# A two-layer SSD and attention network on one core: one block for all stages, ordered by the detailed simulator, and context products by twos

## The chip, the core and the metric

The program runs on one core of a Trainium2 chip. The core has a matrix engine (TensorE, PE in the profile, with its weight loads as PEld), a vector engine (VectorE, DVE), a scalar engine (ScalarE, ACT), a general engine (GpSimd, POOL) and SyncE (SP), which here only issues DMA. Each engine takes its instructions in the order in which the build put them and waits at semaphores for the others. The metric is the device time of one execution, in microseconds (us).

## The reference

The kernel computes two layers of a backbone for 1024 latent tokens and 256 context tokens of width 1024, in float32. Each layer modulates its normalised input (scale, shift and gate from a product with `ada_w`), mixes the tokens, adds the gated result, and does the same with a mixture of experts.

- Layer 0 mixes by a bidirectional state-space scan (SSD): `in_w` projects to a gate z, to x, B and C (a depthwise convolution of width 5 and SiLU behind it) and to step sizes dt. Over chunks of 128 tokens, forwards and backwards, each of 32 heads has `y = (C Bᵀ · decay) x + C · state`, and `state = decay · state + Bᵀ x`; the output is `rmsnorm((y + D x) · silu(z)) @ out_w`. B and C are shared by 4 heads each (8 groups).
- Layer 1 mixes by attention: 16 query heads over 4 key/value heads of width 64, normalised and rotated, softmax over all 1280 tokens for each block of 128 queries.
- The mixture: 16 experts choose their tokens by a router's softmax (128 latent tokens each, 32 context tokens each), and for them `(silu(x w1) · (x w3)) w2`, weighted and added back. Layer 1 has it for latent tokens only.

The output is the normalised latent stream.

## The kernel before

Large products use a three-part form. `mm3` (L54 to L56) multiplies a high and a low part of the operands, high x high, high x low, low x high, into one PSUM tile; the parts are made by a copy on ScalarE (L48, L716) and a subtraction on VectorE or GpSimd (L49, L717, L719). Small products (transposes, scores, the scan's states, context tokens) are done in plain float32 (two passes of the array, so a plain product has two records in the profile).

The stages follow each other in `run`: `constants`, `ssd`, `ssd_out`, `moe(0, True)`, `attn`, `moe(1, False)`. Which instruction stands where on an engine is decided by the language's scheduler, which takes the code in its written order and with that the dependences, the tile pools' buffers and its own costs.

*SSD.* `conv_tile` loads 128 columns of `in_w` (`w_raw`, L323), splits them (L325, L328), projects all tokens in three blocks of 256, 512 and 512 (`in_ps`, L54 to L56), copies them (L351, L352) and applies the convolution (L356) and SiLU (L361, L362). For each of the 8 groups there is one such tile of B, one of C and two of x; each of the two x tiles holds a pair of heads, so the scan runs 16 times (`core`). One run, called a head pair here, transposes x (L371, `xtm`), makes the backward states (L404, with steps on VectorE L390), and then, two chunks at a time: loads the decays' exponents (`Eb`, L413), masks them (GpSimd L416), takes exponentials (ScalarE, 8 of L421), adds and multiplies them (L424, L425); weights x (L378), makes the forward states (L437) with steps (L390); multiplies the entering states by C (`yo_ps`, L450), scales them (`yos`, L454) and adds both directions on GpSimd (L457); and sums the parts of y on TensorE (L465, L467) and stores (L471). Before the groups come the norms, the weights of the modulation (`adw`, L119) and the part that makes dt (L256, L261).

*Mixture 0.* For each expert and each of its three matrices `product` runs over four k (256 rows of the weights each). A k loads 1 MB into a ring of five raw buffers (`m_raw`, L650), splits it, and runs 12 three-part products into `acc` (L54 to L56). The 32 context tokens are multiplied by the raw weights in plain float32: `ctx_part`, 8 products into `cacc` (L690). Where neither the first nor the last product of the stage is meant, this comes at the end of every k. It is the last reader of the raw buffer.

*Attention.* A unit (`Pair`) is two heads by 128 queries; 64 units are written out in an interleaved order. `score` makes the scores of one head, 1024 columns in `S[hh]` and 256 in `S3` (L1129), the maxima (L1133, L1137, L1138) and two exponentials (L1139 for the 256, L1141 for the 1024). `flip` transposes the probabilities (L1150) and copies them (L1155 on ScalarE, L1153 on VectorE), `values` multiplies them (L1163), `close` brings the sums in (L1173 to L1180).

Of the kernel before, what the change touches and what calls it, by code (L numbers as in the profile page):

```python
# [40 lines left out]
class Net:  # L41
# [626 lines left out]
    def moe(self, i, ctx):  # L668

        nc, tc, A = self.nc, self.tc, self.A  # L670
# [6 lines left out]
        with tc.tile_pool(name="mo", bufs=1) as mp, \  # L677
# [9 lines left out]
            def ctx_product(acc, xc, raw, kp):  # L687
                for k in (2 * kp, 2 * kp + 1):
                    for q in range(4):
                        nc.tensor.matmul(acc[32 * q:32 * q + 32], xc[:, k], raw[:, k % 2, 256 * q:256 * q + 256],  # L690
                                         start=(k == 0), stop=(k == KT - 1))

            def product(m, e, xl, xc, done=None):

                acc = [pp.tile([P, 512], F32, name="acc", bufs=5 if ctx else 6) for _ in range(2)]
                cacc = pp.tile([P, 256], F32, name="cacc", bufs=1) if ctx else None
                raws = {}

                def ctx_part(kp):
                    ctx_product(cacc, xc, raws[kp], kp)  # L700
                first = ctx and (m, e) == (0, 0)

                early = ctx and (m, e) == (2, E - 1)
                late = None
                for kp in range(4) if early else ():
                    raws[kp] = self.moe_raw(i, m, e, kp)
                    ctx_part(kp)
                if early:
                    done(cacc)
                for kp in range(4):  # L710
                    n = D - (D if i and m + e == 0 and kp < 3 else share)
                    if not early:
                        raws[kp] = self.ahead.pop(0) if self.ahead else self.moe_raw(i, m, e, kp)
                    raw = raws[kp]
                    w = [wp.tile([P, 2, D], F32R, name=f"m_w{k}", bufs=3) for k in range(2)]
                    nc.scalar.activation(w[0], raw, AF.Copy)  # L716
                    nc.gpsimd.tensor_tensor(w[1][:, :, n:], raw[:, :, n:], w[0][:, :, n:].bitcast(F32), op=OP.subtract)  # L717
                    if n:
                        nc.vector.tensor_tensor(w[1][:, :, :n], raw[:, :, :n], w[0][:, :, :n].bitcast(F32), op=OP.subtract)  # L719
                    for kk in range(2):  # L720
                        k = 2 * kp + kk
                        for b in range(2):
                            self.mm3(acc[b], [h[:, k] for h in xl], [h[:, kk, 512 * b:512 * b + 512] for h in w],
                                     k == 0, k == KT - 1)
                    if first and kp == 1:
                        self.rt.pp, self.rt.tag = pp, "m_tr"
                        self.rt.finish_ctx(self.ctx_rank)
                        self.rk.release()
                        self.hlp = tc.alloc_tile_pool(name="hl", bufs=2, side="right")
                        self.wkvp = tc.alloc_tile_pool(name="wkv", bufs=1, side="right")  # L730
                        self.wkv = [self.wkvp.tile([P, KT, 512], F32R, name=f"wkv{k}") for k in range(2)]
                        self.prep = tc.alloc_tile_pool(name="pre", bufs=1, side="right")
                        late = gather_ctx(0)
                    elif ctx and not first and not early:
                        ctx_part(kp)
                if first:
                    xc = turn_ctx(late)
                    for kp in range(4):
                        ctx_part(kp)
                if done and not early:  # L740
                    done(cacc)
                if m < 2:
                    next(extra, None)
                return acc, cacc
# [18 lines left out]
            def gather_ctx(e):  # L763
                return fetch(mp.tile([32, D], F32, name="xgc"), 0, self.idxC[0:32, e:e + 1]) if ctx else None
# [7 lines left out]
            def turn_ctx(xgc):  # L772
                if xgc is None:
                    return None
                ps = pp.tile([P, KT, 32], F32, name="m_tr", bufs=2)
                for j in range(KT):
                    nc.tensor.transpose(ps[:, j], xgc[:, j * P:(j + 1) * P], self.ident[0:32, 0:32])
                xT = mp.tile([P, KT, 32], F32, name="xTc")
                nc.vector.tensor_copy(xT, ps)
                self.xT = xT  # L780
                return xT
# [29 lines left out]
            def finish(e, gT):  # L811

                y, _ = product(2, e, gT, None)
                fw = slot()[:, 0]
                nc.sync.dma_start(fw, rows(A["final_norm_w"], [0, P], [1, D]))
# [36 lines left out]
            def down(e, gT, gc):  # L852
                y, _ = product(2, e, gT, gc, (lambda yc: scatter_ctx(e, yc)) if ctx else None)
                yr = mp.tile([P, D], F32, name="yrow")
                for b in range(2):
                    hs = slice(512 * b, 512 * b + 512)
                    nc.vector.scalar_tensor_tensor(yr[:, hs], y[b], self.gL[:, e:e + 1], g2[:, hs],
                                                   op0=OP.mult, op1=OP.mult)
                nc.gpsimd.indirect_dma_start(
                    out=self.xs[1], out_offset=bass.IndirectOffsetOnAxis(ap=self.idxL[:, e:e + 1], axis=0),  # L860
                    in_=yr, in_offset=None, compute_op=OP.add)
# [8 lines left out]
            for e in range(E):  # L870
                nx = gather(e + 1) if e + 1 < E else None
                nxc = gather_ctx(e + 1) if 0 < e < E - 1 else None
                a, ac = product(0, e, x, self.xT)
                s = mp.tile([P, D], F32, name="s")
                for b in range(2):
                    nc.scalar.activation(s[:, 512 * b:512 * b + 512], a[b], AF.Silu)
                sc = None
                if ctx:
                    sc = mp.tile([P, 256], F32, name="s_c")
                    nc.scalar.activation(sc, ac, AF.Silu)  # L880
                if e == 0:
                    nxc = gather_ctx(1)
                g, gc = product(1, e, x, self.xT)
                for b in range(2):
                    nc.vector.tensor_tensor(s[:, 512 * b:512 * b + 512], s[:, 512 * b:512 * b + 512], g[b], op=OP.mult)
                if ctx:
                    nc.vector.tensor_tensor(sc, sc, gc, op=OP.mult)
                if ctx and e == E - 2:
                    self.qkv_weights(self.wkv, 2, mp, 2)
                if nx:  # L890
                    x = turn(nx)
                    turn_ctx(nxc)
                if gT:
                    down(e - 1, *gT)
                gT = turn_g(s), turn_gc(sc)
# [368 lines left out]
    def run(self):  # L1264
        nc, tc = self.nc, self.tc
        with ExitStack() as es:
            self.constants(es)
            self.xs, self.h2d = ([tc.dram_tile([n, D], F32, name=f"{nm}{n}") for n in (CTX, LAT)] for nm in ("xs", "h2"))
            self.ssd()
            self.ssd_out()  # L1270
            self.moe(0, True)
            self.attn()
            self.moe(1, False)
            self.rtp.release()


class Router:
# [183 lines left out]
```

## Time and profile before

| | us |
|---|---|
| three runs | 3951.53, 3958.86, 3960.98 (median 3958.86) |
| profiled execution | 3960.7 |
| its span in the trace | 3958.9 |

| engine | busy us | share of the span |
|---|---|---|
| TensorE | 3617.8 | 91% |
| VectorE | 2645.7 | 67% |
| ScalarE | 2030.6 | 51% |
| GpSimd | 1809.5 | 46% |

The stages, as read from the lines at work, are: 0 to 62 us norms and the first modulation; 62 to 140 dt; 140 to 1045 the groups of the SSD; 1045 to 1260 its gates; 1260 to 1525 its output and the router; 1525 to 2390 mixture 0; 2390 to 2595 the projections of the attention; 2595 to 3114 its units; 3114 to 3255 its output and the router; 3255 to 3340 the ranking; 3340 to 3900 mixture 1; then the end. A stage's own row says which engine works through it, and its idle time is the length less the busy time. Records of TensorE overlap a little (0.40 us long, 0.23 apart), so distances are taken from start to start.

### The profile page before, as it was taken

How to read it: one execution, taken by the hardware profiler on the slowest of the kernel's cores; microseconds unless marked ns; L12 is line 12 of the kernel's file. 1: busy time of each engine (PE TensorE's matmuls, PEld its weight loads, DVE VectorE, ACT ScalarE, POOL GpSimd, SP SyncE). 2: the span in 40 equal slices, each digit the busy share in tenths (PEclk: the TensorE clock that was granted, in tenths of full speed). 3: DMA queues.
4: the chain of work that ended last, by engine and by line, in shares of the span. 5: the costliest groups of instructions: out<-in, count | busy, mean ns of one | idle time of the engine just before them, and what ended most of it. 6: DMA issues, size and time to landing. Idle time of an engine off the chain costs nothing.

```text
span 3958.9 us, 56801 instructions
## 1 busy us (share of the span) xinstructions
PE 3617.8 (91%) x21153; PEld 2676.8 (68%) x21153; DVE 2645.7 (67%) x3877; ACT 2030.6 (51%) x3325; POOL 1809.5 (46%) x1370
## 2 busy tenths in 40 slices
PE   5998989999999998999999998999999874999997
PEld 3666777777787775666666666767777653777765
DVE  4777777777633367666666655556666577999988
ACT  4544445444433224554554545477777433777665
POOL 1245545545543224665566663221111123777786
PEclk7999999999999999999999999999999986999999
DMA  4333322222544336889988873100000335999994
GB/s 170 102 102 116 125 81 77 77 77 73 154 143 147 118 128 228 304 298 307 308 298 299 272 248 100 39 17 1 1 1 12 128 129 208 387 375 375 350 335 173
DMA packets 296357, 681.09 MB, mean 172 GB/s; under 512 B 24192, under 2 KB 150000, under 8 KB 289936
## 3 DMA queue, kind: packets, MB, share of 16 engines
q1 hardware_dynamic: 269520, 615.50, 44.5%
q0 software_dynamic: 12720, 39.33, 4.1%
q10 hardware_dynamic: 13840, 22.63, 1.7%
q8 instruction: 167, 2.74, 0.3%
q14 instruction: 110, 0.90, 0.1%
HBM read 611.95 MB, written 62.82 MB: 170 GB/s over the span
## 4 chain that ended last, share of the span: by engine, by line
PE 50%; DVE 15%; issue 7%; POOL 5%; DMA 4%; ACT 3%; SPq 0%; POOLq 0%; ACTq 0%; DVEq 0%
DVE m_w L719 6%; PE acc L54 5%; PE cacc L690 5%; PE pv L1163 4%; PE acc L55 4%; PE acc L56 4%; PE S L1129 4%; PE a_tr L1150 4%; POOL m_w L717 3%; PE in_ps L54 2%; PE in_ps L55 2%; PE in_ps L56 2%; PE o_ps L56 2%; PE o_ps L55 2%; PE o_ps L54 2%
## 5 line engine op out<-in xcount | busy, mean ns | idle before, releaser
L719 DVE TENSOR_TENSOR m_w<-m_raw,m_w 128x1792 fp32r<-128x1792 f32 (+1 forms) x381 | 877.1, 2323 | 323.3 <-ACT m_w L716 320.8
L717 POOL TENSOR_TENSOR m_w<-m_raw,m_w 128x256 fp32r<-128x256 f32 (+1 forms) x384 | 859.5, 2248 | 403.5 <-ACT m_w L716 401.4
L716 ACT ACTIVATE m_w<-m_raw 128x2048 fp32r<-128x2048 f32 x384 | 732.4, 1915 | 493.3 <-PE acc L56 210.1
L54 PE MATMUL in_ps<-hh,w 128*128 128x512 f32 (+1 forms) x1152 | 429.3, 373 | 9.9 <-DVE th L493 9.9
L55 PE MATMUL acc<-m_w,xl 128*128 128x512 f32 x1024 | 409.1, 400 | 19.0 <-DVE m_w L719 12.4
L56 PE MATMUL in_ps<-hh,w 128*128 128x512 f32 (+1 forms) x1152 | 425.5, 369 | 0.0
L55 PE MATMUL in_ps<-hl,w 128*128 128x512 f32 (+1 forms) x1152 | 424.4, 368 | 0.0
L54 PE MATMUL acc<-m_w,xl 128*128 128x512 f32 x1024 | 412.9, 409 | 2.6 <-ACT xl L48 1.7
L56 PE MATMUL acc<-m_w,xl 128*128 128x512 f32 x1024 | 401.8, 393 | 0.0
L421 ACT ACTIVATE Eb<-Eb,ebias 128x128 f32<-128x128 f32 x640 | 201.8, 391 | 191.0 <-POOL Eb L416 191.0
L1133 DVE TENSOR_REDUCE mx<-S 128x1 f32<-128x1024 f32 x128 | 155.7, 1217 | 183.5 <-PE S L1129 183.5
L328 POOL TENSOR_TENSOR w<-w_raw,w 128x512 fp32r<-128x512 f32 x96 | 151.5, 1596 | 253.8 <-ACT w L325 245.5
L54 PEld LDWEIGHTS acc<-m_w,xl 128*128 128x128 f32 x1024 | 192.8, 189 | 91.8 <-issue 42.9
L54 PEld LDWEIGHTS in_ps<-hh,w 128*128 128x128 f32 x1152 | 221.6, 192 | 47.5 <-issue 11.8
L56 PEld LDWEIGHTS in_ps<-hh,w 128*128 128x128 f32 x1152 | 221.2, 192 | 38.1 <-issue 12.8
L55 PEld LDWEIGHTS in_ps<-hl,w 128*128 128x128 f32 x1152 | 221.5, 192 | 36.8 <-issue 12.0
L55 PEld LDWEIGHTS acc<-m_w,xl 128*128 128x128 f32 x1024 | 193.7, 189 | 77.0 <-DVE m_w L719 26.5
L1180 POOL TENSOR_TENSOR q<-s 64x128 f32<-64x128 f32 x128 | 57.6, 450 | 405.9 <-DVE mx L1138 338.0
L56 PEld LDWEIGHTS acc<-m_w,xl 128*128 128x128 f32 x1024 | 193.5, 189 | 40.2 <-DVE xl L49 0.2
L55 PE MATMUL acc<-m_w,gT 128*128 128x512 f32 x512 | 205.3, 401 | 6.6 <-DVE m_w L719 4.1
L54 PE MATMUL acc<-m_w,gT 128*128 128x512 f32 x512 | 206.9, 410 | 1.0 <-ACT gT L48 1.0
L56 PE MATMUL acc<-m_w,gT 128*128 128x512 f32 x512 | 201.0, 393 | 0.1
(382 smaller groups left out, 7747.3 us busy)
## 6 DMA issues: line engine op xcount, KB each, us to landing
m_raw<-in_moe_w_dram SPq DMA_DIRECT2D x384, 1024.0 KB
adw<-in_ada_w_dram SPq DMA_DIRECT2D x48, 1024.0 KB
Eb<-fd SPq DMA_DIRECT2D x80, 512.0 KB
w_raw<-in_ssd_in_w_dram SPq DMA_DIRECT2D x48, 512.0 KB
ydd<-yd SPq DMA_DIRECT2D x80, 128.0 KB
yt_raw<-yzd SPq DMA_DIRECT2D x40, 256.0 KB
xs<-x SPq DMA_DIRECT2D x16, 512.0 KB
h<-h SPq DMA_DIRECT2D x16, 512.0 KB
```

The source lines that it names most:

```text
L54: mm(out, lhs[0], rhs[0], start=start, stop=False)
L55: mm(out, lhs[0], rhs[1], start=False, stop=False)
L56: mm(out, lhs[1], rhs[0], start=False, stop=stop)
L421: nc.scalar.activation(Eb[:, d, hh, cc], Eb[:, d, hh, cc], AF.Exp, bias=bias[:, c0 + cc, k:k + 1])
L690: nc.tensor.matmul(acc[32 * q:32 * q + 32], xc[:, k], raw[:, k % 2, 256 * q:256 * q + 256], start=(k == 0), stop=(k == KT - 1))
L716: nc.scalar.activation(w[0], raw, AF.Copy)
L717: nc.gpsimd.tensor_tensor(w[1][:, :, n:], raw[:, :, n:], w[0][:, :, n:].bitcast(F32), op=OP.subtract)
L719: nc.vector.tensor_tensor(w[1][:, :, :n], raw[:, :, :n], w[0][:, :, :n].bitcast(F32), op=OP.subtract)
L1129: nc.tensor.matmul(o, qTs[self.qt][:, 2 * self.hp + hh], kT[k][:, self.kv, 512 * b:512 * b + n], start=(k == 0), stop=(k == 1))
L1133: nc.vector.tensor_reduce(self.mx[:, 0:1], S[hh], axis=AX.X, op=OP.max)
L1150: nc.tensor.transpose(ps[:, q], self.pr[hh][:, (c0 + q) * P:(c0 + q + 1) * P], net.ident)
L1163: nc.tensor.matmul(self.pv[o:o + 64, 0], v32[:, t, self.kv], self.PT[:, t], start=(t < 2), stop=(t >= NT - 2))
```

## The change

Two edits. In `product`, the context products of an even k now wait for the odd one, and both stand behind the odd k's three-part products. In `run`, all stages lie in one block that is scheduled with the build's timeline simulator; the constants stay ahead of it, in a block of their own.

```diff
-                    elif ctx and not first and not early:
+                    elif ctx and not first and not early and kp % 2:
+
+                        ctx_part(kp - 1)
                         ctx_part(kp)
...
-            self.ssd()
-            self.ssd_out()
-            self.moe(0, True)
-            self.attn()
-            self.moe(1, False)
-            self.rtp.release()
+
+            with tc.block(schedule_with_timeline_sim=True):
+                self.ssd()
+                self.ssd_out()
+                self.moe(0, True)
+                self.attn()
+                self.moe(1, False)
+                self.rtp.release()
```

Lines behind the first edit move down by two, from L736 to L1268 of the kernel before.

On SyncE, at the program's start, these are the loads of the kernel before:

```order
L73 DMA cr<-in_c_dram 128x8
L74 DMA cr<-in_c_ctx_dram 128x8
L119 DMA adw<-in_ada_w_dram 128x2048 x3
L190 DMA xx<-in_ctx_dram 128x2x1024
L190 DMA xx<-in_x_dram 128x2x1024 x3
```

and these of the changed one:

```order
L73 DMA cr<-in_c_dram 128x8
L74 DMA cr<-in_c_ctx_dram 128x8
L1272 UNCONDITIONAL_BRANCH
L190 DMA xx<-in_ctx_dram 128x2x1024
L119 DMA adw<-in_ada_w_dram 128x2048
L190 DMA xx<-in_x_dram 128x2x1024
L119 DMA adw<-in_ada_w_dram 128x2048
L190 DMA xx<-in_x_dram 128x2x1024
L119 DMA adw<-in_ada_w_dram 128x2048
```

The three loads of the modulation's weights stood ahead of the inputs; now they stand between them, behind the branch into the new block.

On TensorE, in the SSD groups, within the chain of a late head pair (`st_ps` is the state product, `yo_ps` the entering one, `y_ps` the output; `in_ps` is a projection of a later tile), before:

```order
L437 MATMUL st_ps<-xw_8970,Btm 128x128
L467 MATMUL y_ps<-ident,yos 128x128
L465 MATMUL y_ps<-Eb,xtm 64x128 x2
L450 MATMUL yo_ps<-H_8943,CT 128x128
L467 MATMUL y_ps<-ident,yos 128x128
L437 MATMUL st_ps<-xw_8970,Btm 128x128
L450 MATMUL yo_ps<-H_8853,CT 128x128
L56 MATMUL in_ps<-hh,w_9230 128x512
L54 MATMUL in_ps<-hh,w_9229 128x512
L465 MATMUL y_ps<-Eb,xtm 64x128 x2
L55 MATMUL in_ps<-hl,w_9229 128x512
L437 MATMUL st_ps<-xw_9019,Btm 128x128
```

and of the same chain now:

```order
L450 MATMUL yo_ps<-H_8975,CT 128x128
L450 MATMUL yo_ps<-H_8854,CT 128x128
L437 MATMUL st_ps<-xw_9020,Btm 128x128
L467 MATMUL y_ps<-ident,yos 128x128
L465 MATMUL y_ps<-Eb,xtm 64x128 x4
L450 MATMUL yo_ps<-H_8979,CT 128x128
L450 MATMUL yo_ps<-H_8854,CT 128x128
L437 MATMUL st_ps<-xw_9020,Btm 128x128
L467 MATMUL y_ps<-ident,yos 128x128
L450 MATMUL yo_ps<-H_9024,CT 128x128
L450 MATMUL yo_ps<-H_8854,CT 128x128
L437 MATMUL st_ps<-xw_9069,Btm 128x128
```

The projections (L54 to L56) that stood within the chain are gone from it; they stand in one piece ahead of it or behind it.

On TensorE in mixture 0, the end of one k and the context products behind it, before:

```order
L56 MATMUL acc<-m_w_14489,xl_14110 128x512
L54 MATMUL acc<-m_w_14489,xl_14109 128x512
L55 MATMUL acc<-m_w_14490,xl_14109 128x512
L56 MATMUL acc<-m_w_14489,xl_14110 128x512
L690 MATMUL cacc<-m_raw,xTc 32x256 x8
```

and now:

```order
L56 MATMUL acc<-m_w_15209,xl_14962 128x512
L54 MATMUL acc<-m_w_15209,xl_14961 128x512
L55 MATMUL acc<-m_w_15210,xl_14961 128x512
L56 MATMUL acc<-m_w_15209,xl_14962 128x512
L690 MATMUL cacc<-m_raw,xTc 32x256 x16
```

The context products stand in runs of 16 (two k) with 24 three-part products between them, before in runs of 8 with 12.

On ScalarE in the attention, one unit (`pr` are probabilities of `S`, `PT` their transposed copies, `s` the sums), before:

```order
L1155 ACTIVATE PT<-a_tr 128x4x128
L1139 ACTIVATE pr,sm<-S_21318,mx 128x256
L1141 ACTIVATE pr,sm<-S_21317,mx 128x1024
L1139 ACTIVATE pr,sm<-S_21318,mx 128x256
L1141 ACTIVATE pr,sm<-S_21316,mx 128x1024
L1155 ACTIVATE PT<-a_tr 128x2x128
L1155 ACTIVATE PT<-a_tr 128x4x128
L1155 ACTIVATE PT<-a_tr 128x2x128
L1175 ACTIVATE s_24103<-pv 64x256
L1176 ACTIVATE s_24103<-pv 64x256
L1155 ACTIVATE PT<-a_tr 128x4x128
```

and now:

```order
L1157 ACTIVATE PT<-a_tr 128x2x128
L1141 ACTIVATE pr,sm<-S_21319,mx 128x256
L1143 ACTIVATE pr,sm<-S_21318,mx 128x1024
L1157 ACTIVATE PT<-a_tr 128x4x128
L1157 ACTIVATE PT<-a_tr 128x2x128
L1141 ACTIVATE pr,sm<-S_21319,mx 128x256
L1143 ACTIVATE pr,sm<-S_21317,mx 128x1024
L1157 ACTIVATE PT<-a_tr 128x4x128
L1177 ACTIVATE s_24189<-pv 64x256
L1178 ACTIVATE s_24189<-pv 64x256
L1157 ACTIVATE PT<-a_tr 128x2x128
```

Before, the two pairs of exponentials stand next to each other. Now two copies of transposed pieces, and in the other place a copy, the two sums and a copy, stand between them.

## Rows read from the trace of the kernel before

**Rows 1.** Busy by stage: stretch, length, PE, PEld, DVE, ACT, POOL, PEclk, DMA, GB/s.

```profile
62.00:140.00 78.00, 54.40 (x253) 41.45 (x254) 45.81 (x71) 21.32 (x34) 10.09 (x17) 0.82 0.21 62
140.00:1045.00 905.00, 819.57 (x4878) 640.45 (x4876) 654.13 (x1328) 418.95 (x1041) 448.25 (x518) 0.98 0.30 95
...
1525.00:2390.00 865.00, 846.95 (x6016) 550.39 (x6015) 529.47 (x454) 437.08 (x332) 528.11 (x269) 0.99 0.85 287
...
2595.00:3114.00 519.00, 513.94 (x3494) 370.46 (x3493) 309.67 (x687) 389.11 (x906) 85.30 (x144) 1.00 0.01 4
```

**Rows 2.** Instructions of PE from 1699 us: start, length, instruction.

```profile
1700.53 0.39 PE L55 MATMUL acc<-m_w,xl 128*128 128x512 f32 x1
1700.76 0.39 PE L56 MATMUL acc<-m_w,xl 128*128 128x512 f32 x1
1701.08 1.07 PE L690 MATMUL cacc<-m_raw,xTc 128*32 128x256 f32 x16
1702.08 0.50 PE L54 MATMUL acc<-m_w,xl 128*128 128x512 f32 x1
1702.42 0.40 PE L55 MATMUL acc<-m_w,xl 128*128 128x512 f32 x1
```

**Rows 3.** The same, a long block of context products.

```profile
2371.95 3.66 PE L690 MATMUL cacc<-m_raw,gTc 128*32 128x256 f32 x64
2375.54 0.50 PE L56 MATMUL acc<-m_w,gT 128*128 128x512 f32 x1
```

**Rows 4.** Waits in 1640 to 2360 us: in total, times, longest.

```profile
ACT m_w L716 <- DMA m_raw<-in_moe_w_dram: 63.3, 28, 4.1
...
SPq L650 <- PE cacc L690: 621.7, 166, 6.3
```

**Rows 5.** DMA issues of SP at the start: start, length.

```profile
1.66 2.11 SPq L119 DMA_DIRECT2D adw<-in_ada_w_dram  x3
9.71 0.38 SPq L190 DMA_DIRECT2D xx<-in_ctx_dram  x1
```

**Rows 6.** Waits of PE over the span.

```profile
PE r_tr L1310 <- DVE h L1333: 13.5, 9, 7.1
```

**Rows 7.** Instructions of DVE in a chain of the SSD groups.

```profile
881.81 0.78 DVE L425 TENSOR_TENSOR Eb<-Eb,cb 128x512 f32<-128x512 f32 x1
883.07 0.47 DVE L390 SCALAR_TENSOR_TENSOR H<-H,dec,st_ps 128x64 f32<-128x64 f32 x2 [0.47 <-PE st_ps L437]
883.46 0.42 DVE L454 TENSOR_TENSOR yos<-yo_ps,eF 128x256 f32<-128x256 f32 x1
883.79 0.41 DVE L378 TENSOR_TENSOR xw<-xtm,wst 128x256 f32<-128x256 f32 x1
...
885.27 0.47 DVE L471 SCALAR_TENSOR_TENSOR yd<-xT,dcol,y_ps 128x256 f32<-128x256 f32 x1
```

**Rows 8.** Groups of ACT, 700 to 925 us: count, busy and mean, idle before.

```profile
L421 ACT ACTIVATE Eb<-Eb,ebias 128x128 f32<-128x128 f32 x160 | 50.7, 391 | 39.8 <-POOL Eb L416 39.8
```

**Rows 9.** Two waits of PE, and the clock behind the first.

```profile
843.20 2.08 PE L515 MATMUL tr_ps<-CT,BT 128*128 128x128 f32 x8 [3.61 <-DVE CT L362]
...
843.00:848.80 5.80, 5.60 (x22) 5.12 (x22) 2.18 (x4) 1.92 (x4) 1.80 (x4) 0.50 0.00 0
...
880.84 0.49 PE L437 MATMUL st_ps<-xw,Btm 128*128 128x128 f32 x2 [0.57 <-DVE H L390]
```

**Rows 10.** Attention: groups of ACT, 2604 to 3104 us; instructions of PE.

```profile
L1141 ACT ACTIVATE pr<-S,mx 128x1024 f32<-128x1024 f32 x122 | 134.8, 1105 | 0.0
...
L1139 ACT ACTIVATE pr<-S,mx 128x256 f32<-128x256 f32 x122 | 57.6, 472 | 40.5 <-DVE rs L1167 40.0 <-DVE mx L1138 0.3
L1155 ACT ACTIVATE PT<-a_tr 128x256 f32<-128x256 f32 x122 | 46.7, 383 | 56.2 <-PE a_tr L1150 56.2
...
2819.37 1.18 PE L1129 MATMUL S<-kT,qT 128*128 128x512 f32 x4
2820.39 1.04 PE L1150 MATMUL a_tr<-ident,pr 128*128 128x128 f32 x8
```

## The prediction

> **What bounds the kernel now.** I read the busy time by stage first. TensorE is the engine to follow: it works 820 of the 905 us of the SSD groups, 847 of the 865 us of the first mixture stage and 514 of the 519 us of the attention, each at a granted clock of 0.98 to 1.00 of full speed; in the first stretch after the start (62 to 140 us) it works only 54 of 78 [rows 1]. So what the change can win lies in three places: the idle 85 us of the SSD groups, the idle 24 of the stretch before them, and whatever TensorE does not need to do. Next I read its instructions one by one, for what a change of kind costs. Two products of the three-part form (L54 to L56, 128x512) start 0.23 us apart (1700.53, 1700.76). The short products behind them start 0.32 later instead, and the first two of the next three-part run 0.34 apart (1702.08, 1702.42) [rows 2]. One excursion into another kind thus costs about (0.32 − 0.23) + (0.34 − 0.23) = 0.20 us beside its own work.
>
> **The twos.** A context block of one k has 16 records and takes 1.00 us (1701.08 to 1702.08) [rows 2]; a block of 64 took 3.59 us (2371.95 to 2375.54) [rows 3]. Split as a fixed part and a part per 16, that is 0.137 + 0.863 per 16. Putting two blocks together saves the fixed part once and one excursion: 0.137 + 0.20 = 0.337 us. In the new order the number of excursions in this stage, counted in the instruction order of both programs, falls from 205 to 121, so 84 pairs are real: 84 x 0.337 = 28 us. Nothing else covers this, since TensorE is busy through the stage. Against it stands the ring of raw weights: SP waits 622 us, 166 times, for a context block before it may issue the next load [rows 4], because that block is the last reader of a slot. The even k's slot now comes free one product (about 4 us) later. ScalarE, which makes the first part of the split weights, waits 63 us for the load already [rows 4], 28 times, and these do not reach TensorE now. The bounds are −28 (all hidden) and 0 (the late slot eats the gain); I take −24, near the end that the rows of TensorE give: five slots at 4 us each leave 20 us from one use of a slot to the next; a load of 1.05 MB at the stage's 287 GB/s [rows 1] takes 3.7 of them, and of what splitting, the products of two k and the late block leave, I count some 2 us as slack.
>
> **One block: the start.** In the kernel before, the first three weight loads are issued at 1.66 us and the first input at 9.71 [rows 5]. The constants now stand in a block of their own, the weights behind the input: the stream starts about 8 us later. VectorE also makes all 18 high parts of the inputs before the 18 low parts, which I put at 7 us by counting them. That is +15. TensorE, however, is idle for about 24 of the 78 us in which the step sizes dt are made [rows 1]; the new order puts three-part products of the first projections into these gaps, 24 to 33 in a run. I take 20 of the 24. Start: −5 (from −20 to +15).
>
> **One block: the SSD groups.** Excursions fall from 374 to 120: 254 x 0.20 = −51 us. The price is in the shape that buys it: the projections of a head pair's tile are run ahead in one piece, and the pair's chain of chunks (state product, step, entering product, scaling, sum, output) then stands with none of them in between. In the chain VectorE has, for one head pair, 9 pairs of steps (0.47 each), 10 scalings of the entering states (0.42), 5 weightings (0.41), 5 outputs (0.47) and 5 products of decays (0.78) [rows 7]: 4.2 + 4.2 + 2.1 + 2.4 + 3.9 = 16.8, of which about 2 us (the first weighting, the first two products of decays) are done before the chain starts. With hops between engines the chain is 15 to 17 us, TensorE's part in it 9.7 (my count of its products at the spacing of such products in the trace). So TensorE idles some 6.3 us in each of 16 chains: 101 us. Behind the chain, one more wait: ScalarE holds 16 exponentials of the next pair (16 x 0.39 = 6.3) [rows 8] ahead of the copy that frees the projection's PSUM; I count 3.75 us of it as uncovered, 8 times: 30 us. These 131 replace the 85 idle now: +46. To this comes the clock.
>
> [...] I count 15 us: five of the eight long stalls. The groups: −51 + 46 + 15 = +10, from −60 (idle as now, clock as now, plus part of the 85) to +60.
>
> [...]
>
> **One block: the attention.** It has 128 wide exponentials, two to a unit; 122 of them lie in 500 us, so a unit takes 8.2 us [rows 10], all of it TensorE's. The new order moves the last 256 columns of the second half's scores to the unit's end, straight ahead of the next unit's scores, and ScalarE copies the next unit's first transposed piece before that half's exponentials. From the end of these scores to the next use of their PSUM: four score products and two transposes (1.5 with the correction), a copy 0.38, the narrow exponential with its read-out 0.66, the wide one 1.3, hops 0.3: 4.1 us. TensorE has in that time the same 1.5, then eight transposes (1.04) [rows 10], the narrow scores and two transposes, 3.3 in all. It waits 0.5 to 0.9 us in each unit, and saves 1.5 excursions (0.3). Net +0.26 x 64 = +17, from −19 (no wait, excursions saved) to +40.
>
> **The rest.** The router's transposes behind the SSD output stood where TensorE waited 13.5 us for them [rows 6]; the new order puts them about 22 products later: −4 there and −5 after the attention by the same move, where the tail without cover gives some back (0 to −15 together). The second mixture stage is bound by its loads and its order hardly differs: 0 (±8).
>
> **Sum.** −24 − 5 + 10 + 17 − 9 = −11 on the profiled execution's 3960.7 us: 3949.7. It lies 1.8 us over the median of the runs, 3958.9, so the forecast is 3948 us.
>
> **Rivals.** A, faster: the chains are not as bare as I count them. The engines' queues let one pair's head overlap the tail of the one before, half of the added idle (23) and of the clock loss (8) go, and the attention's waits only eat the saved excursions (−17): 3948 − 48 = 3900. For it speaks that TensorE is given 51 us less to do; against it that no projection stands within a chain. B, slower: the clock falls behind every chain and stall, at 2.6 us each for 24 places, 62 instead of 15 (+47), and the attention's wait is 0.85 instead of 0.56 (+18): 3948 + 65 = 4013. [...] C: the twos do nothing, since the raw weights come late; −24 becomes 0: 3972.
>
> **How the numbers follow.** A measurement here can tell 0.3%, 12 us, from no change. Forecast 0.38, with its own range 3925 to 3975 (0.17 faster, 0.17 the same, 0.04 slower); A 0.26, all faster; B 0.26, all slower; C 0.10, half the same and half slower. Faster 0.43, same 0.22, slower 0.35. The range reaches to the middle of A and just over that of B: 3895 to 4020.
>
> **What would show it.** Right: in the mixture stage, half as many context blocks, each about 1.87 us, and 24 us less in the stage. In the groups, TensorE busy about 50 us less, with long waits for the entering scaling or for the steps, each near a chain, and granted clock below 0.98. In the attention, a wait of the scores for the exponentials of 0.5 us or more in each unit. First three-part product later by 15 us. Wrong: waits of under 3 us per chain (then A), a granted clock of 0.9 in the groups (then B), ScalarE's wait for raw weights well over 63 us and reaching TensorE (then C), or an attention unit under 8.2 us.

## The result and the profile after

The changed kernel takes 4080.0 us in the median (4071.7 to 4090.7, 4 runs), the kernel before 3957.2 (3951.5 to 3961.0, 4 runs): 1.0313 times as long, 95% interval 1.0284 to 1.0342. The forecast was 3948 with a range of 3895 to 4020: wrong in sign, and outside its range. The profiled execution has a span of 4069.9 us, 111.0 more than the one of before.

The stages are cut here at TensorE's own instructions (first projection, first backward state, last output product, first product of the SSD output, and so on), the same cut in both traces; each difference is of two such lengths.

| stage | before | after | difference | forecast |
|---|---|---|---|---|
| start to first projection | 75.7 | 86.7 | +11.0 | +15 |
| first projection to first scan | 93.3 | 142.2 | +48.9 | −20 |
| SSD groups (first scan to last output) | 877.6 | 910.0 | +32.4 | +10 |
| gates | 209.9 | 208.0 | −1.9 | 0 |
| SSD output, router | 279.0 | 290.3 | +11.3 | −4 |
| mixture 0 | 852.3 | 830.3 | −22.0 | −24 |
| projections of the attention | 181.3 | 179.7 | −1.6 | 0 |
| attention units | 544.0 | 572.7 | +28.7 | +17 |
| output of the attention, router | 135.0 | 114.2 | −20.8 | −5 |
| ranking, mixture 1, end | 710.9 | 735.7 | +24.8 | 0 |

Three of the ten decide: the two of the SSD (+81 together) and the attention (+29). Mixture 0 came out near its forecast. After the attention 21 us are gained and 25 given back.

The page of the changed kernel opens with the span and the busy times:

```profile
span 4069.9 us, 56856 instructions
...
PE 3616.7 (89%) x21153; PEld 2749.4 (68%) x21153; DVE 2596.7 (64%) x3877; ACT 2006.5 (49%) x3325; POOL 1773.4 (44%) x1370
...
PEclk7979998899899999999999998999999996999998
```

TensorE is busy as long as before (3617.8 there) although it changes between kinds of product far less often. The row of the clock gives one reason: three of the slices in the second and third tenth of the span, in the SSD groups, have an eight, where the kernel before has nines.

The same stages as in [rows 1], by the windows view of the changed kernel (columns as there; the first is from the first projection to the first scan, then groups, mixture 0, attention, its output, and ranking with mixture 1):

```profile
86.70:228.90 142.20, 121.81 (x604) 94.97 (x605) 84.63 (x117) 54.78 (x101) 27.26 (x34) 0.90 0.19 56
...
228.90:1138.90 910.00, 788.37 (x4524) 634.69 (x4522) 592.11 (x1275) 386.56 (x973) 368.39 (x498) 0.89 0.29 91
1637.20:2467.60 830.40, 813.78 (x5982) 563.25 (x5983) 519.10 (x429) 421.22 (x315) 515.84 (x262) 0.99 0.83 294
2647.30:3220.10 572.80, 526.15 (x3575) 369.08 (x3573) 339.11 (x706) 380.87 (x937) 96.25 (x151) 1.00 0.02 6
3220.10:3334.20 114.10, 107.41 (x551) 82.21 (x555) 65.08 (x97) 34.88 (x77) 16.98 (x8) 0.96 0.51 185
3334.20:4045.10 710.90, 593.39 (x2665) 474.32 (x2664) 600.61 (x509) 431.64 (x323) 506.24 (x226) 0.93 0.84 307
```

The groups and the attention units of the kernel before, cut at the same instructions:

```profile
169.00:1046.60 877.60, 792.16 (x4750) 623.16 (x4749) 635.25 (x1299) 401.55 (x998) 446.78 (x512) 0.98 0.31 95
```

```profile
2569.00:3113.00 544.00, 529.35 (x3575) 381.31 (x3573) 327.05 (x710) 404.53 (x938) 96.19 (x150) 0.99 0.02 6
```

In the groups TensorE's idle time is 122 us (before, between the same two instructions, 85), and the granted clock is 0.89 where it was 0.98. The clock's record in both traces holds 1.00 and 0.50 and nothing else (94 entries here, 62 before); of the 910 us 203 lie at 0.50, here called half clock, against 41 before.

How a chain ends shows where the halves come from. TensorE of the changed kernel, in the last third of one head pair's chain (start, length, instruction, idle before it and what ended it):

```profile
859.35 0.71 PE L450 MATMUL yo_ps<-H,CT 128*128 128x128 f32 x4
859.90 0.39 PE L437 MATMUL st_ps<-xw,Btm 128*128 128x128 f32 x2
860.12 0.39 PE L467 MATMUL y_ps<-ident,yos 128*128 128x128 f32 x2
860.65 0.71 PE L450 MATMUL yo_ps<-H,CT 128*128 128x128 f32 x4
861.19 0.39 PE L437 MATMUL st_ps<-xw,Btm 128*128 128x128 f32 x2
863.77 0.49 PE L467 MATMUL y_ps<-ident,yos 128*128 128x128 f32 x2 [2.19 <-POOL yos L457]
864.19 0.44 PE L465 MATMUL y_ps<-Eb,xtm 128*64 128x128 f32 x4
864.56 0.71 PE L450 MATMUL yo_ps<-H,CT 128*128 128x128 f32 x4
...
865.86 1.21 PE L450 MATMUL yo_ps<-H,CT 128*128 128x128 f32 x4 [0.36 <-DVE yos L454]
868.47 0.69 PE L465 MATMUL y_ps<-Eb,xtm 128*64 128x128 f32 x4 [1.40 <-DVE Eb L425]
869.09 0.80 PE L467 MATMUL y_ps<-ident,yos 128*128 128x128 f32 x2
```

and the windows view of the same place:

```profile
859.00:866.00 7.00, 4.31 (x35) 3.27 (x31) 3.17 (x12) 2.79 (x10) 3.54 (x7) 0.99 0.53 174
865.90:876.10 10.20, 8.47 (x37) 6.34 (x38) 6.16 (x13) 7.75 (x23) 6.33 (x9) 0.50 0.41 126
```

The longest single wait ahead of the low clock is 2.19 us. Then, at 0.50, four records of entering products take 1.21 us instead of 0.71. The low clock lasts 10.2 us, over the end of this chain and the start of the next (whose first state products stand at 873.24 us).

In the attention the forecast wait is there (45 times in the 64 units, 26.8 us in the view of waits) and of the forecast size:

```profile
2900.92 0.50 PE L1131 MATMUL S<-kT,qT 128*128 128x256 f32 x2
2902.01 1.21 PE L1131 MATMUL S<-kT,qT 128*128 128x512 f32 x4 [0.59 <-ACT pr L1143]
...
2910.02 0.50 PE L1131 MATMUL S<-kT,qT 128*128 128x256 f32 x2
2911.11 1.20 PE L1131 MATMUL S<-kT,qT 128*128 128x512 f32 x4 [0.59 <-ACT pr L1143]
```

The two starts are 9.1 us apart, a unit with the preparation of the next queries in it ([rows 10] gave 8.2 in the mean).

### The profile page after: what moved, and what is told of

Its sections match the earlier page's. It is cut to its first block, busy times and chain, and to the rows that moved or that the text cites. A ratio compares the mean times of both kernels' runs of the same rounds, so it can differ in the third digit from the quotient of the medians.

```text
span 4069.9 us, 56856 instructions
## 1 busy us (share of the span) xinstructions
PE 3616.7 (89%) x21153; PEld 2749.4 (68%) x21153; DVE 2596.7 (64%) x3877; ACT 2006.5 (49%) x3325; POOL 1773.4 (44%) x1370
## 5 line engine op out<-in xcount | busy, mean ns | idle before, releaser
L719 DVE TENSOR_TENSOR m_w<-m_raw,m_w 128x1792 fp32r<-128x1792 f32 (+1 forms) x381 | 842.0, 2221 | 299.7 <-ACT m_w L716 298.3
L54 PE MATMUL in_ps<-hh,w 128*128 128x512 f32 (+1 forms) x1152 | 427.5, 371 | 8.7 <-DVE th L493 8.1
L55 PE MATMUL acc<-m_w,xl 128*128 128x512 f32 x1024 | 407.1, 398 | 16.8 <-DVE m_w L719 14.4
L56 PE MATMUL in_ps<-hh,w 128*128 128x512 f32 (+1 forms) x1152 | 420.8, 365 | 0.0
L56 PE MATMUL acc<-m_w,xl 128*128 128x512 f32 x1024 | 403.6, 396 | 0.0
L54 PE MATMUL acc<-m_w,xl 128*128 128x512 f32 x1024 | 386.9, 401 | 10.7 <-ACT xl L48 9.8
L54 PEld LDWEIGHTS in_ps<-hh,w 128*128 128x128 f32 x1152 | 229.7, 199 | 45.2 <-DVE th L493 9.4
L56 PEld LDWEIGHTS in_ps<-hh,w 128*128 128x128 f32 x1152 | 228.3, 198 | 33.6 <-issue 4.4
L54 PEld LDWEIGHTS acc<-m_w,xl 128*128 128x128 f32 x1024 | 194.1, 190 | 75.3 <-issue 13.2
L56 PEld LDWEIGHTS acc<-m_w,xl 128*128 128x128 f32 x1024 | 194.5, 191 | 39.4
L1152 PE MATMUL a_tr<-ident,pr 128*128 128x128 f32 x1280 | 197.3, 279 | 14.0 <-DVE PT L1155 9.6
L55 PE MATMUL acc<-m_w,gT 128*128 128x512 f32 x512 | 202.4, 395 | 7.8 <-DVE m_w L719 7.4
L56 PE MATMUL acc<-m_w,gT 128*128 128x512 f32 x512 | 200.3, 392 | 1.9 <-DVE gT L49 1.9
L1152 PEld LDWEIGHTS a_tr<-ident,pr 128*128 128x128 f32 x1280 | 146.9, 141 | 73.3 <-ACT PT L1157 15.4
```

Source lines behind the costliest of these rows:

```text
L54: mm(out, lhs[0], rhs[0], start=start, stop=False)
L55: mm(out, lhs[0], rhs[1], start=False, stop=False)
L56: mm(out, lhs[1], rhs[0], start=False, stop=stop)
L1152: nc.tensor.transpose(ps[:, q], self.pr[hh][:, (c0 + q) * P:(c0 + q + 1) * P], net.ident)
```

## The experiments

**The order or the block?** Two kernels. The first has the twos alone, in the kernel before:

```diff
-                    elif ctx and not first and not early:
+                    elif ctx and not first and not early and kp % 2:
+                        ctx_part(kp - 1)
                         ctx_part(kp)
```

> The context products by twos alone, in the kernel before, no block. My sum: 92 pairs at most and 0.337 us saved by each, so the first mixture stage is about 24 us shorter (852 to 828 us from its first product to the first transpose of the attention's projections) and the whole 0.6% faster than before (about 3933 us). Rival (the late block starves the ring of raw weights): no change within 0.3%, ScalarE's wait for raw weights well over 63 us.

The second is the changed kernel with the block, but the usual scheduler in it:

```diff
-            with tc.block(schedule_with_timeline_sim=True):
+            with tc.block():
```

> As the changed kernel, but the block is ordered by the usual scheduler, not by the timeline simulator. If the order is what costs, this runs as the twos alone plus the later start (the weights' loads stand behind the input): 3933 + 8 to 15, so 0.993 to 0.998 of before, with granted clock 0.96 or more. Rival: the block as such (its barrier, the split of the constants) costs most of the 123 us: above 4020 us.

Measured: 3916.9 us for the twos, 0.9898 of before (0.9882 to 0.9915); 3919.7 for the plain block, 0.9898 (0.9882 to 0.9915). In the same order, mixture 0 of the twos and the groups and units of the plain block:

```profile
1530.60:2346.40 815.80, 797.56 (x5982) 558.19 (x5983) 524.20 (x433) 424.61 (x317) 510.73 (x265) 1.00 0.84 301
```

```profile
170.10:1047.20 877.10, 793.69 (x4750) 623.86 (x4749) 638.30 (x1299) 402.70 (x998) 443.38 (x512) 0.97 0.30 95
2532.30:3076.30 544.00, 529.58 (x3575) 381.82 (x3573) 327.02 (x710) 404.50 (x938) 96.13 (x150) 0.99 0.02 6
```

The twos take 36.5 us out of the stage (852.3 to 815.8), more than forecast, and the block as such costs no more than some 3 us: with it the groups and the units are as long as before (877 and 544). The order that the timeline simulator finds costs the whole difference between 3920 and 4080 us. The twos alone are faster than both kernels.

**What the twos are worth inside the block.** The changed kernel without the twos, in a single run:

```diff
-                    elif ctx and not first and not early and kp % 2:
-                        ctx_part(kp - 1)
+                    elif ctx and not first and not early:
                         ctx_part(kp)
```

> The block with the simulator's order, context products as before (one k each). What the twos are worth inside the block: if the twos alone make the changed kernel's first mixture stage shorter, the stage is 845 to 860 us here, against 830 in the changed kernel and 852 before, and the whole some 15 to 25 us above the changed kernel. Rival: the simulator's order shortens the stage by itself (816 to 835 us).

4092.7 us, and mixture 0 is 855.6 us, 25 more than with the twos (830.3) and 3 more than before: within the block too it is the twos that shorten the stage. But the simulator's order leaves only 54 blocks of two whole k unbroken, the twos alone 91.

**Is it the clock?** The changed kernel with more work. The entering product of the backward state (`H1`) waits for nothing within the chain, so it can fill a gap; it is done three times instead of once.

```diff
-                    for d in dd:
+                    for d in (1, 1, 1, 0) if len(dd) == 2 else dd:
                         nc.tensor.matmul(yo[:, cc, d], CT[:, c * P:(c + 1) * P], (ent[cc], H1[:, c])[d],
                                          start=True, stop=True)
```

> As the changed kernel, but in each chunk of a chain that has both directions the entering product of the backward state, which waits for nothing in the chain, runs three times instead of once (same values; the order around it stays nearly that of the changed kernel). That is 16 products more for a head pair, some 0.2 us each: 55 us of work for TensorE in all. Theory (a chain without projections lets the clock fall, and that is the larger part of the loss): with the gaps filled the time at half clock in the groups falls from 204 us to under 150, and the groups (910 us) grow by less than 20 or shrink. Rival (the low clock comes from the stretches behind the chain, where nothing is ready): half clock stays at 190 to 220 us, and the groups grow by 20 to 60.

4067.8 us, 1.0262 of before (1.0245 to 1.0279), against 1.0313 for the changed kernel (1.0284 to 1.0342). The groups:

```profile
227.20:1134.70 907.50, 814.81 (x5036) 668.88 (x5034) 612.63 (x1275) 384.80 (x973) 376.37 (x498) 0.94 0.29 91
```

TensorE with the added products, at full clock:

```profile
850.62 1.16 PE L450 MATMUL yo_ps<-H,CT 128*128 128x128 f32 x8
851.62 0.39 PE L437 MATMUL st_ps<-xw,Btm 128*128 128x128 f32 x2
```

There are 5036 − 4524 = 512 records more, 256 products. Eight records take 1.00 us from start to start (850.62 to 851.62), four took 0.55 (859.35 to 859.90 in the changed kernel): 0.45 us for two products more, so 57 us of work are added. The stretch is 2.5 us shorter. The time at half clock fell from 203 to 115 us, TensorE's busy time within it from 161 to 102, and the idle time from 122 to 93. I count the clock's price on the busy time alone, since idle time at half clock is idle time already: half of the 60 us that are no longer worked at half clock is 30 us, and with 29 us of idle time filled that is 59 us, about what the added work costs.

By the same count (161 us worked at half clock against 39 before) the clock's price in the changed kernel's groups is (161 − 39) / 2 = 61 us. This is an upper end: the same four records of L465 take 0.62 us at half clock (868.47 to 869.09) and 0.37 at full (864.19 to 864.56), 1.7 times and not twice, by which it would be 50.

The run supports that the low clock is a cause of the loss and not only a sign of it, but it does not isolate the clock. The simulator ordered the kernel anew, and some 12% of TensorE's other records in the groups stand in another order; and a chain that another engine bounds would also have taken in the added work without growing. Against this second reading stands the comparison by the eight groups, each cut at its first backward state product: where the work at half clock fell most (by 18 us) the group is 6.6 us shorter, where it rose (by 1.7 us) 5.4 us longer (the correlation over the eight is 0.77), while the idle time fell by 1 to 5 us in each.

**Projections back into the chain.** The changed kernel, with the products of the next tile queued behind the state products of the running chain:

```diff
+        anchors = []
...
             for k in range(KT):
-                self.mm3(ps[:, :n], [w[m][:, k] for m in range(2)], [hT(m, k, b) for m in range(2)],
-                         k == 0, k == KT - 1)
+                at = anchors[(8 * b + k) * len(anchors) // 24] if anchors else None
+                with (tc.issue_after(at) if at is not None else ExitStack()):
+                    self.mm3(ps[:, :n], [w[m][:, k] for m in range(2)], [hT(m, k, b) for m in range(2)],
+                             k == 0, k == KT - 1)
+            if b == 2 and anchors:
+                anchors[:] = anchors[-1:]
...
-                    nc.tensor.matmul(ps[:, cc], Btm[:, c], xw[:, cc], start=True, stop=True)
+                    anchors.append(nc.tensor.matmul(ps[:, cc], Btm[:, c], xw[:, cc], start=True, stop=True).ins)
...
+            anchors.clear()
             M, ent, yos = {}, {}, {}
```

> As the changed kernel, but the projection of the next tile is queued on TensorE by thirds of a block behind the state products of the running chain, so that 9 three-part products stand between two steps again (the order's number of excursions rises by about 140 in the groups, +28 us by my price). Theory (the groups lose by the low clock of bare chains): the stretch from the first projection to the last output product falls from 1052 us to about 985, granted clock there from 0.89 to 0.95 or more, busy time of TensorE from 910 to about 870; the whole about 4010 us. Rival (VectorE's steps bound the chain, the clock is only a sign): the clock rises, but the idle time grows by as much, and the stretch stays within 1035 to 1060 us.

4180.8 us, 1.0559 of before (1.0541 to 1.0577): slower by another 2.5%, which neither theory had. The windows view, the first row within the main part of one chain and the second from its end to the next chain:

```profile
620.00:640.00 20.00, 20.00 (x130) 16.60 (x128) 10.40 (x31) 7.09 (x22) 7.67 (x12) 1.00 0.23 73
641.00:669.00 28.00, 13.26 (x56) 9.58 (x56) 19.74 (x36) 9.64 (x24) 15.61 (x15) 0.58 0.27 84
```

and TensorE behind it:

```profile
641.14 0.71 PE L456 MATMUL yo_ps<-H,CT 128*128 128x128 f32 x4 [0.29 <-DVE yos L460]
646.58 0.80 PE L473 MATMUL y_ps<-ident,yos 128*128 128x128 f32 x2 [4.73 <-POOL yos L463]
...
651.13 0.80 PE L473 MATMUL y_ps<-ident,yos 128*128 128x128 f32 x2 [3.13 <-POOL yos L463]
653.24 1.12 PE L377 MATMUL tr_ps<-ident,xT 128*128 128x128 f32 x4 [1.31 <-DVE xT L368]
656.69 1.12 PE L377 MATMUL tr_ps<-ident,xT 128*128 128x128 f32 x4 [2.33 <-ACT xtm L378]
```

Within the chain the aim was met: TensorE busy for all 20 us, at full clock. But the projection of the only tile that stood ready was used up there. The 28 us to the next chain, in which that tile is convolved, turned and its backward states are made, are now bare, half idle and mostly at half clock. There are 292 us at half clock in the groups and 217 idle. The groups take 1048.4 us instead of 910.0, of which 30 come back ahead of the first scan (199.3 us instead of 228.9). The cover of a head pair is a fixed amount, and what is moved to one place is missing at another; the kernel before has it spread over both.

**The attention.** The changed kernel, with TensorE's instructions in a unit pinned to their written order:

```diff
+            def pin_(f, *x, **k):
+                return tc.keep_in_program_order(f(*x, **k))
...
-                        nc.tensor.matmul(o, qTs[self.qt][:, 2 * self.hp + hh], kT[k][:, self.kv, 512 * b:512 * b + n],
+                        pin_(nc.tensor.matmul, o, qTs[self.qt][:, 2 * self.hp + hh], kT[k][:, self.kv, 512 * b:512 * b + n],
...
-                        nc.tensor.transpose(ps[:, q], self.pr[hh][:, (c0 + q) * P:(c0 + q + 1) * P], net.ident)
+                        pin_(nc.tensor.transpose, ps[:, q], self.pr[hh][:, (c0 + q) * P:(c0 + q + 1) * P], net.ident)
...
```

> As the changed kernel, but TensorE's instructions in the attention's units are kept in their written order (each behind the one traced before). Theory (the last scores at the unit's end, ahead of a copy and the exponentials, cost 0.5 us in a unit): the stage from first scores to the output's first product falls from 573 to about 544 us, as before, and the whole by 29 us to about 4050. Rival (ScalarE's order, which stays the simulator's, is what costs): the stage stays within 565 to 580 us.

4045.5 us, 1.0221 of before (1.0203 to 1.0238). The units take 547.5 us instead of 572.7 (544.0 before), 25 of the 29 lost. The wait of the scores for the wide exponential is gone (26.8 us to 2.3); in its place stand short ones of the transposes, 33 us in all:

```profile
PE a_tr L1116 <- ACT PT L1160: 29.7, 90, 0.5
PE a_tr L1116 <- DVE PT L1158: 3.0, 4, 1.2
```

```profile
2647.80:3195.30 547.50, 508.69 (x3571) 372.64 (x3569) 324.79 (x705) 396.19 (x937) 96.04 (x150) 1.00 0.02 6
```

So the length is what the theory expected, but not by its mechanism alone: of the 25 us only 8 are idle time (46.7 to 38.8 us), and 17 are busy time of TensorE (526.1 to 508.7). What in the pinned order saves the busy time was not taken apart.

**All four k together.** The twos taken further, in the kernel before:

```diff
-                    elif ctx and not first and not early and kp % 2:
-                        ctx_part(kp - 1)
-                        ctx_part(kp)
+                    elif ctx and not first and not early and kp == 3:
+                        for q in range(4):
+                            ctx_part(q)
```

> The twos alone, without a block, but the context products of all four k of a product stand behind its last k. By the measured price of a pair (0.447 us saved) another 46 x 0.45 = 20 us would go from the first mixture stage (816 to 796 us), the whole to 3897. Rival (the ring of five raw buffers now starves: four of them are held until the last k, and ScalarE waits 247 us for raw weights already): the stage grows, to 830 us or more, with TensorE waiting for split weights.

3981.6 us, 1.0045 of before (1.0031 to 1.0058), and the stage takes 872 us. The stage is slower, as the rival had it, but for the most part not by its mechanism: of the 56 us more than with the twos 10 are idle time (28 us, with the twos 18), the rest is busy time. The usual scheduler broke most blocks of 64 records into pieces of 2 to 54:

```profile
1916.74 1.05 PE L690 MATMUL cacc<-m_raw,xTc 128*32 128x256 f32 x10
...
1920.68 0.64 PE L690 MATMUL cacc<-m_raw,xTc 128*32 128x256 f32 x8
...
1923.75 0.62 PE L690 MATMUL cacc<-m_raw,xTc 128*32 128x256 f32 x6
```

The stage has 172 runs of context products, where the twos have 99, so this run is no test of the ring.

## Why the prediction was wrong

**The step that failed is the clock's, and with it the credit for fewer excursions.** The two stretches of the SSD were to give −10 us and gave +81. Of the 91 us between, the clock makes 36 to 47, the excursions 30 to 41 and the idle time 14.

*The clock.* I counted 15 us for the groups, on one row: a wait of 3.61 us in one piece [rows 9], with the assumption that only waits of that kind lower the clock. No run shows that term. What the runs show in its place, by the time worked at half clock, is 50 to 61. Of the 23 pieces at half clock that begin in the changed kernel's groups, 21 have no wait of more than 3.0 us within 12 us ahead of them; the longest is mostly about 2 us (1.7 to 2.6 in 20 of them; at the last, at 1080.9 us, it is 2.97, and one of 4.40 begins 0.1 us behind the start). The other two, at 237.8 and 261.7 us, stand at waits of 3.7 and 3.6 us. So no wait as long as that of the row stood ahead of those 21, but shorter ones in a chain of short products, and the low clock then lasted 3.4 to 24 us, over the chain's own work. The trace of before has this too, and I did not use it: one of its ten half-clock pieces in the groups begins at 268.7 us, and the waits ahead of it, back to 256 us, are one of 2.6 and one of 1.0 us.

```profile
268.70:272.10 3.40, 3.19 (x12) 2.90 (x13) 2.16 (x5) 0.60 (x1) 0.17 (x3) 0.50 0.52 143
```

**The projections run ahead.** I let them fill the gaps of the start and booked −20. The idle time ahead of the first scan did not fall by 20 us, it rose from 16.7 to 20.4: the simulator's order runs the projections of later tiles ahead of the first scan (+49 until it starts), and the groups, with that much less left to do, still take 32 us more. The cover was spent where little needed it. Over both stretches the idle time grew by 40 us (my net 26: +46 in the groups, −20 ahead of them), and the time worked at half clock by 124, some 51 to 62 us; with the measured +81 this leaves −10 to −21 for the excursions, where I had −51. Their price of 0.20 us was read in mixture 0; by the same reckoning the excursions in the groups of the kernel before cost about 0.15 us each, which would still give some −39. Where the rest went stays open. So of the terms of the SSD the idle time was near, the clock was three to four times too small and the saving more than twice too large. Rival B had the clock fall behind every chain and stall and priced that at 62 us, about what the clock cost; I gave it 0.26. Its 2.6 us for each of 24 places was an estimate that no run shows: the trace has 23 pieces, of 3.4 to 24 us. Its 4013 is still 67 us short, above all because it kept my saving and my −20.

**The twos: right, and too small by a quarter.** The block of two k takes 1.86 us (1.87 forecast). The period of a pair fell from 2 x 3.987 to 7.527 us, by 0.447 instead of 0.337, and 91 such pairs give 41 us (the stage gave 36.5, since TensorE's idle time in it also rose by 7 us): besides the excursion and the fixed part, the three-part products stand 228 ns apart instead of 231, 24 of them in a pair. In the changed kernel 22 us are left of it, since its order breaks the blocks. That this lies so near my 24 is luck in part: I counted 84 pairs at 0.337 us, and 54 whole pairs at 0.447 make 24. My sign for trouble was a bad one: ScalarE's wait for raw weights rose from 63 us to 247 and did not reach TensorE (which waits 1.0 us for ScalarE's part in this stage in both kernels).

```profile
ACT m_w L716 <- DMA m_raw<-in_moe_w_dram: 247.3, 104, 6.3
```

**The attention: the mechanism was right, the credit wrong.** The wait is 0.6 us, within my 0.5 to 0.9, and TensorE's idle time in the stage rose by 32 us, 0.5 in each unit; 27 of them are this wait. What did not come is the 0.3 us per unit for fewer excursions: its busy time fell by 3 us in all.

**The routers.** I booked −4 behind the SSD from a wait that the view gave for the whole span [rows 6]; in that stage it was 5.6 us, and moving the transposes later left the ranking without cover. At the stage's end TensorE waits 10.4 and 9.4 us for it:

```profile
PE r_tr L1374 <- DVE lg L1368: 10.4, 1, 10.4
PE r_lg L1405 <- DVE idf L1403: 9.4, 1, 9.4
```

After the attention the same move gave −21 in the output's stage and was lost again in the stage behind it (+25 to the end), which begins with the ranking. That the ranking's chain is what gives it back there was not tried alone; the waits for it rose from 39.9 to 45.7 us in the longest.

**The start** was late by 11.0 us (15 forecast). The plain block, with the same split of the constants, is late by 3.3: the first input goes out at 5.6 us, not 9.7 as in [rows 5], so the split costs less than I said, and the simulator's order of the rest costs the other 8.

## What to carry to other kernels

In these runs TensorE's waits cost more than their length where they were many (in the changed kernel's groups 122 us of idle time stand beside 203 us at half clock, in those of the kernel before 85 beside 41): list the pieces at half clock and look what precedes each, before pricing an order that packs short dependent products together. Long independent products were a fixed stock of cover here; an order that saves changes of kind by running them in one piece takes the cover from the chains, and one that puts them all into the chain takes it from what lies between (217 us idle in the groups of that run, 122 in the changed kernel's). When a change has a local part and a global reordering, price and try them apart: here the local part alone gave 1.0% and the reordering took 4%.

## What was not expected of the hardware

Adding 57 us of products to TensorE's chains left the groups 2.5 us shorter (910.0 to 907.5), the time at half clock falling from 203 to 115 us. And where two short blocks were grouped, the products around them also stood closer together (231 to 228 ns; why is not shown), so that a pair gave 0.447 us instead of the 0.337 that its edges showed.
